# Experts of a decoder block: a float32 second layer from unsplit weights, and 64 rows for the lesser expert of a pair

## The chip, the cores and the metric

One core of a Trainium2 chip runs the whole program; the other cores are idle. The metric is the device time of one execution in microseconds (us), as the median of three runs. Lower is better. The engines are called PE (matrix multiplication), DVE (vector), ACT (scalar), POOL (GpSimd) and SP (which issues most transfers); PEld is PE's loading of stationary operands.

## The reference, cut to what matters

One decoder block on 512 tokens of width 1024: a gated delta-net branch and a dilated attention branch are merged, then comes a mixture of 64 experts, of which each token uses 8, and one shared expert. The change touches the experts alone.

```
scores = sigmoid(h @ w_router); choose 8 experts of each token; wk = their scores, normalised, * 2.5
a = einsum('td,edf->tef', h, w_gate)          # h (512, 1024), w_gate and w_up (64, 1024, 256)
u = einsum('td,edf->tef', h, w_up)
routed = einsum('tef,efd->td', silu(a) * u * combine[..., None], w_down)   # w_down (64, 256, 1024)
out = x + gt2 * (routed + shared)
```

All arrays are float32. An expert's three matrices are 1 MiB each, so that the 64 experts bring 192 MiB (201 MB) from memory in an execution.

## The kernel before, in words

**Precision.** A float32 operand that PE is to multiply is split into a part `hi` of type float32r (a rounded copy, ACT) and a rest `lo` (DVE or POOL, `raw - hi`). A product is then three float32r matmuls: hi·hi, hi·lo and lo·hi. Both layers of an expert work so, lines 1841 to 1843 for the first (gate and up side by side, 512 columns, 8 steps of k, 24 matmuls) and lines 1854 to 1856 for the second (two halves of 512 columns, 2 steps of k, 12 matmuls).

**Jobs.** `make_jobs` (L1657) lays out 36 jobs of up to 128 gathered rows. Experts 0 and 1 have a job each. The other 62 are ranked by their number of tokens, and the most wanted is paired with the least wanted, and so on. The six pairs with the most rows are served by three *triples* of jobs, each with 4 experts and 6 runs of an expert; the other 25 pairs by one job each, with 2 runs. That is 70 runs of an expert (called entries here) with 64 experts' weights. In a pair's job all 128 rows go through both experts, and a row's weight is zero for the expert that it doesn't use.

**The loop.** `run` (L1858) goes through the entries. In entry e PE does, in this order: for the last entry of a job, the eight transposes of the next job's gathered rows (`tile_rows`, L1816); the first five k steps of the first layer; the two transposes of the *previous* entry's result (`mid`, which calls `turned`, L1628); the last three steps; then the second layer of the previous entry (`finish`, `down`, L1846). `turned` writes the transposed result from PSUM twice: ACT copies it to float32r (`hi`) and DVE subtracts to get `lo`, both on line 1638. `gated` (L1620) makes the result from the first layer's PSUM: silu on ACT (L1624), and a product on DVE (L1625).

**Weights.** An expert has six loads of 128x1024 from SP's queue, in order, each into one of ten raw buffers (`raw_tile`). Each part is then cast by ACT and subtracted: first layer L1781 and L1785 (of its four parts one on POOL, three on DVE), second layer L1800 and L1801 (both on DVE). A raw buffer is free for a load when its subtraction is over. The split first-layer weights have two sets of buffers (`wt`, `wy`) for alternate experts, the second layer has two sets as well. The first-layer parts of the second half (j = 1) are split in `mid`, behind `turned`, from the fourth expert on (L1787).

**Rows.** `tile_slot` makes the table of rows of a job: four comparisons with an iota that give one-hots (`slot`, L1649), and four small matmuls (L1653). For the first jobs DVE does the comparisons, from job 6 on POOL does. POOL also issues the gather of rows (L1807) and the scatter that adds a job's result to the output (L1813). `pair_rows` (L1381) gives the rows of a pair their positions, the lesser expert's first.

At the end `overflow` (L2097) runs further jobs, if an expert has more rows than its jobs hold; with these inputs none are needed.

```
au = self.gate_up(x[n], w, mid)
th = self.gated(sw, au, slots[n][1][:, s : s + 1])
if e >= 2 and final[flat[e - 2][2]] == e - 2:
    weights(self.down_weights, flat[e - 2][2] + 2)
if final[w] == e:
    weights(self.gate_up_weights, w + 2)
```

## Time and profile before

| | |
|---|---|
| runs | 1628.46 us median of 3 (1626.53 to 1633.29) |
| the profiled execution | 1629.41 us, its span 1627.6 us |
| PE, PEld busy | 1503.0 us (92%), 1288.1 us (79%) |
| DVE, ACT, POOL busy | 1162.5 us (71%), 847.6 us (52%), 614.2 us (38%) |
| mean granted clock of PE | 0.964 of full speed |
| moved | 344.93 MB, mean 212 GB/s |

A matmul's duration in the profile covers its way through the engine: matmuls overlap, and what one costs in a row of its kind is the distance from its start to the next one's start. A wait is put down to the instruction that ended it. The expert loop begins at 915 us and is the last part of the program.

### The profile page before, as it was taken

What the parts mean: (1) busy time and instruction counts of PE and PEld (TensorE: products, weight loads), DVE (VectorE), ACT (ScalarE), POOL (GpSimd) and SP (SyncE); (2) the same over time, 40 slices, a digit from 0 to 9 for tenths busy, and PEclk for the clock granted to TensorE, in tenths of its full rate; (3) what the DMA queues carried; (4) which work ended last, traced back from release to release, by engine and by line L of the source; (5) the groups of instructions that cost most, each with busy time, mean ns of one, the idle gap of its engine ahead of it and who ended that gap; (6) DMA issues with size and microseconds to landing.
All of it is one profiled execution on the core that took longest, in us unless ns stands there. A gap on an engine that the chain in (4) does not pass through costs nothing.

```text
span 1627.6 us, 25142 instructions
## 1 busy us (share of the span) xinstructions
PE 1503.0 (92%) x8635; PEld 1288.1 (79%) x8635; DVE 1162.5 (71%) x1918; ACT 847.6 (52%) x1697; POOL 614.2 (38%) x422
## 2 busy tenths in 40 slices
PE   4978889899999999999998999899899999998996
PEld 3667778799999999788888777787777877787885
DVE  6678856586655743433477879978998699879885
ACT  5466243544454444323333366657655676656773
POOL 4343121302111111001104397566835594747442
PEclk7999999999999999999997999999999999999998
DMA  8434331323455544233445799999999899989994
GB/s 281 116 99 117 108 87 33 85 91 94 154 146 167 156 135 132 87 101 106 163 142 195 234 291 350 340 326 312 358 317 336 277 351 367 320 293 309 377 375 150
DMA packets 182864, 344.93 MB, mean 212 GB/s; under 512 B 30915, under 2 KB 120206, under 8 KB 182726
## 3 DMA queue, kind: packets, MB, share of 16 engines
q1 hardware_dynamic: 169254, 300.48, 54.0%
q0 software_dynamic: 12672, 40.61, 10.0%
q10 hardware_dynamic: 800, 2.13, 0.3%
q8 instruction: 70, 1.15, 0.3%
q14 instruction: 68, 0.56, 0.1%
HBM read 319.79 MB, written 28.92 MB: 214 GB/s over the span
## 4 chain that ended last, share of the span: by engine, by line
PE 62%; DVE 16%; issue 7%; DMA 6%; ACT 5%; POOL 4%; SPq 0%; POOLq 0%; DVEq 0%; ACTq 0%
PE ps_mm L164 9%; PE ps_mm L165 9%; PE ps_mm L166 9%; PE ps_sm L1841 6%; PE ps_sm L1842 6%; PE ps_sm L1843 6%; DMA gb<-gcd 3%; PE ps_mm L1856 3%; PE ps_mm L1854 3%; PE ps_mm L1855 3%; PE ps_tp L170 2%; DVE lo L1801 2%; PE ps_sm L170 2%; DVE wt L1785 1%; DMA rx<-in_w_exp_up_dram 1%
## 5 line engine op out<-in xcount | busy, mean ns | idle before, releaser
L164 PE MATMUL ps_mm<-hi,hhi 128*128 128x256 f32 x704 | 206.8, 294 | 0.0
L166 PE MATMUL ps_mm<-hi,hlo 128*128 128x256 f32 x704 | 199.8, 284 | 0.0
L165 PE MATMUL ps_mm<-lo,hhi 128*128 128x256 f32 x704 | 199.6, 284 | 0.0
L146 DVE TENSOR_TENSOR lo<-raw,hi 128x1024 fp32r<-128x1024 f32 (+1 forms) x92 | 113.7, 1244 | 109.1 <-ACT hi L144 108.9
L1649 POOL TENSOR_SCALAR oh<-iota,tb 128x128 bf16<-128x128 bf16 x120 | 155.4, 1471 | 0.5
L144 ACT CAST hi<-raw 128x1024 fp32r<-128x1024 f32 (+1 forms) x104 | 103.8, 1014 | 73.7 <-PE ps_mm L165 73.1
L164 PEld LDWEIGHTS ps_mm<-hi,hhi 128*128 128x128 f32 x704 | 135.0, 192 | 3.6 <-PE ps_mm L287 1.3
L1856 PE MATMUL ps_mm<-hi,sw 128*128 128x512 f32 x280 | 114.1, 410 | 24.4 <-DVE sw L1638 24.4
L165 PEld LDWEIGHTS ps_mm<-lo,hhi 128*128 128x128 f32 x704 | 135.1, 192 | 0.1
L164 PE MATMUL ps_mm<-hhi,hi 128*128 128x512 f32 x320 | 132.0, 413 | 3.4 <-DVE cj L563 3.4
L166 PEld LDWEIGHTS ps_mm<-hi,hlo 128*128 128x128 f32 x704 | 134.9, 192 | 0.0
L166 PE MATMUL ps_mm<-hhi,lo 128*128 128x512 f32 x320 | 128.7, 402 | 0.0
L165 PE MATMUL ps_mm<-hlo,hi 128*128 128x512 f32 x320 | 128.3, 401 | 0.0
L1801 DVE TENSOR_TENSOR lo<-rx,hi 128x1024 fp32r<-128x1024 f32 x82 | 114.2, 1427 | 5.0 <-ACT hi L1800 2.7
L1841 PE MATMUL ps_sm<-wt,xh 128*128 128x512 f32 x280 | 117.0, 418 | 0.2 <-ACT xh L1826 0.2
L1842 PE MATMUL ps_sm<-wy,xh 128*128 128x512 f32 x280 | 111.7, 399 | 5.1 <-POOL wy L1785 5.1
L1841 PE MATMUL ps_sm<-wy,xh 128*128 128x512 f32 x280 | 116.2, 415 | 0.0
L1638 ACT CAST sw<-ps_sm 128x256 fp32r<-128x256 f32 x70 | 26.2, 374 | 170.7 <-PE ps_sm L170 168.7
L1842 PE MATMUL ps_sm<-wt,xh 128*128 128x512 f32 x280 | 111.1, 397 | 3.4 <-POOL wt L1785 3.4
L1854 PE MATMUL ps_mm<-hi,sw 128*128 128x512 f32 x280 | 112.3, 401 | 0.5 <-ACT sw L1638 0.5
L1855 PE MATMUL ps_mm<-lo,sw 128*128 128x512 f32 x280 | 112.2, 401 | 0.0
L1843 PE MATMUL ps_sm<-wy,xl 128*128 128x512 f32 x280 | 111.8, 399 | 0.0
(527 smaller groups left out, 4165.1 us busy)
## 6 DMA issues: line engine op xcount, KB each, us to landing
raw<-in_w_in_dram SPq DMA_DIRECT2D x84, 512.0 KB
rx<-in_w_exp_down_dram SPq DMA_DIRECT2D x82, 512.0 KB
rx<-in_w_exp_gate_dram SPq DMA_DIRECT2D x74, 512.0 KB
rx<-in_w_exp_up_dram SPq DMA_DIRECT2D x74, 512.0 KB
raw<-in_w_exp_gate_dram SPq DMA_DIRECT2D x54, 512.0 KB
raw<-in_w_exp_up_dram SPq DMA_DIRECT2D x54, 512.0 KB
raw<-in_w_exp_down_dram SPq DMA_DIRECT2D x46, 512.0 KB
raw<-in_w_ada_dram SPq DMA_DIRECT2D x40, 512.0 KB
```

Source lines behind the costliest of these rows:

```text
L146: eng.tensor_sub(lo[:, s], raw, hi[:, s].bitcast(F32))
L164: nc.tensor.matmul(out, l[0], r[0], start=(k == 0), stop=False)
L165: nc.tensor.matmul(out, l[0], r[1], start=False, stop=False)
L166: return nc.tensor.matmul(out, l[1], r[0], start=False, stop=(k == kd - 1)).ins
L1649: eng.tensor_scalar(oh[:, i, :], iota, col(i)[0], None, op0=ALU.is_equal)
L1801: nc.vector.tensor_sub(dl[:, s], raw, dh[:, s].bitcast(F32))
L1841: nc.tensor.matmul(o, l[0], r[0], start=(k == 0), stop=False)
L1842: nc.tensor.matmul(o, l[0], r[1], start=False, stop=False)
L1843: nc.tensor.matmul(o, l[1], r[0], start=False, stop=(k == KD - 1))
L1854: nc.tensor.matmul(ps[n], hh[0][:, k, :], r[0], start=first and k == 0, stop=False)
L1855: nc.tensor.matmul(ps[n], hh[0][:, k, :], r[1], start=False, stop=False)
L1856: nc.tensor.matmul(ps[n], hh[1][:, k, :], r[0], start=False, stop=last and k == 1)
```

## The change

1. **Second layer.** The weights of the second layer are loaded as they are, in float32, into one of four buffers (`down_tile`; before: two sets of hi and lo). The transposed result is one float32 copy by ACT. The second layer is 4 float32 matmuls in place of 12 float32r ones. ACT's casts and DVE's subtractions of L1800 and L1801 are gone, and so is DVE's `lo` in `turned`.
2. **Lesser expert.** A pair's lesser expert (31 of the 70 entries, `seconds`) has the first 64 rows of its job. `second_rows` (ACT, two copies) puts hi and lo of these 64 rows side by side in one stationary operand of 128 columns. A step of k is then two matmuls: [hi | lo] by the weights' hi, and hi (64 columns) by their lo, 16 in place of 24. The lower 64 PSUM rows are added to the upper ones in `gated_second`: one copy on ACT and two additions on DVE ahead of silu and product. Its `mid` comes after six steps of k.
3. **No tensor work on POOL.** The subtractions and the comparisons that POOL did go to DVE; POOL keeps the gathers and scatters.
4. **Buffers.** Eight raw buffers, for the four loads of the first layer only (before ten, for six). The second layer's loads go straight into `down_tile`.
5. **Rows.** `pair_rows`, `over_rows` and `extra_table` get some small operations on DVE, for pairs whose lesser expert has more than 64 rows.

```diff
     def rest():
-            xl = late.tile([P, 4, 4, P], F32R, name="xl", tag="mT00", bufs=1)
-            self.fx.tiles["xl"] = [xl[:, x] for x in range(4)]
-            rx = late.tile([P, 2, 1024], F32, name="rx", tag="mT01", bufs=1)
-            self.raws[8:10] = [rx[:, x] for x in range(2)]
+            xx = [late.tile([P, 2, 4, 2, P], F32R, name="xx", tag="mT0%d" % x, bufs=1) for x in range(2)]
+            self.fx.tiles["xx"] = [xx[x // 2][:, x % 2] for x in range(4)]
...
+    def gated_second(self, pools, au, comb):
...
+        both = self.fx.tile([P, T], F32, tag="part")[0:M]
+        nc.scalar.copy(both, au[M : 2 * M])
+        for j in range(2):
+            cs = slice(j * 256, j * 256 + 256)
+            nc.vector.tensor_add(both[:, cs], au[0:M, cs], both[:, cs])
+        self.gate_ins = [nc.scalar.activation(th, both[:, 0:256], AF.Silu).ins,
+                         nc.vector.scalar_tensor_tensor(th, th, comb[0:M], both[:, 256:512], op0=ALU.mult,
+                                                        op1=ALU.mult).ins]
...
     def turned(self, pools, th):
...
+        if rows < P:
+            hh = self.fx.tile([P, 2, P], F32, tag="sw_s")
+            pv = ps[:, 0:256].rearrange("p (j t) -> p j t", t=P)[:, :, 0:rows]
+            self.turn_ins = [nc.scalar.copy(hh[:, :, 0:rows], pv).ins]
+            return hh
+        if len(pools) == 2:
+            p, tag, bufs = pools[1]
+            hh = p.tile([P, 2, P], F32, name="sw_f", tag=tag, bufs=bufs)
+            self.turn_ins = [nc.scalar.copy(hh, ps[:, 0:256].rearrange("p (j t) -> p j t", t=P)).ins]
+            return hh
...
+    def down_tile(self, w):
+
+        t = self.wd
+        if t[w % 4] is None:
+            tag = ("hi8", "lo8")[w % 2]
+            t[w % 4] = self.ring.tile([P, 2048], F32, name="wd", tag=tag, bufs=2)
+        return t[w % 4]
 
     def raw_tile(self):
-        n = self.turn
+        x = self.turn % 8
         self.turn += 1
-        x = self.raw_order[n if n < 16 else 16 + (n - 16) % 10]
...
-                    eng = nc.gpsimd if (self.low_pool.pop(0) if self.low_pool else a == 1 and j == 0) else nc.vector
...
-                        eng.tensor_sub(gl, rv, gh.bitcast(F32))
+                        nc.vector.tensor_sub(gl, rv, gh.bitcast(F32))
...
     def down_weights(self, w, load):
-        nc = self.nc
-        dh, dl = self.weight_set(w, 1)
+        d = self.down_tile(w)
         for j in range(2):
-            s = slice(j * 1024, j * 1024 + 1024)
-            raw = self.raw_tile()
-            load(raw, 2, j)
-            with self.tc.issue_after(self.turn_ins[0]) if w >= 2 else ExitStack():
-                nc.scalar.copy(dh[:, s], raw)
-            nc.vector.tensor_sub(dl[:, s], raw, dh[:, s].bitcast(F32))
+            load(d[:, j * 1024 : j * 1024 + 1024], 2, j)
...
+    def second_rows(self, x):
+
+        xs = [self.fx.tile([P, 4, P], F32R, tag="xs") for _ in range(2)]
+        for kk in range(2):
+            self.nc.scalar.copy(xs[kk].rearrange("p k (s r) -> p k s r", s=2), x[kk][:, :, :, 0:M].bitcast(F32))
+        return xs
...
         for k in range(KD):
-            if k == 5:
+            if k == (6 if second else 5):
                 mid()
...
+            if second:
+                xk = x[k // 4][:, k % 4]
+                parts = [(o, xk, r[0]), (o[0:M], xk[:, 0:M], r[1])]
+                for m, (oo, l, rr) in enumerate(parts if k < KD - 1 else parts[::-1]):
+                    nc.tensor.matmul(oo, l, rr, start=(k + m == 0), stop=(k + m == KD))
+                continue
...
     def down(self, ps, hh, w, first, last):
...
-        for n in range(2):
-            for k in range(2):
+        for k in range(2):
+            for n in range(2):
                 c = k * D + n * 512
-                r = [d[s][:, c : c + 512] for s in range(2)]
-                nc.tensor.matmul(ps[n], hh[0][:, k, :], r[0], start=first and k == 0, stop=False)
-                nc.tensor.matmul(ps[n], hh[0][:, k, :], r[1], start=False, stop=False)
-                nc.tensor.matmul(ps[n], hh[1][:, k, :], r[0], start=False, stop=last and k == 1)
+                nc.tensor.matmul(ps[n], hh[:, k, :], d[:, c : c + 512], start=first and k == 0, stop=last and k == 1)
...
+            if e + 1 < len(flat) and flat[e + 1][2] in seconds and not w in seconds:
+                xs = self.second_rows(x[flat[e + 1][0]])
...
-            au = self.gate_up(x[n], w, mid)
-            th = self.gated(sw, au, slots[n][1][:, s : s + 1])
+            second = w in seconds
+            au = self.gate_up(xs if second else x[n], w, mid, second)
+            th = (self.gated_second if second else self.gated)(sw, au, slots[n][1][:, s : s + 1])
+            if second and e + 1 < len(flat) and flat[e + 1][2] in seconds:
+                xs = self.second_rows(x[flat[e + 1][0]])
...
-                    later.append(self.tile_slot(n + 4, nc.gpsimd))
+                    later.append(self.tile_slot(n + 4, nc.vector))
...
+        seconds = [NS + x for x, u in enumerate(self.pairs) if u >= NQ]
+        self.run([ws for _, ws in self.jobs], prepare, load, ahead, between, seconds)
```

## Rows read from the trace of the kernel before

**Rows 1.** The busy time of each engine in eight stretches (the windows view; the columns stand in its first line). The first seven lie end to end and are the expert loop from the first matmul of job 2 to that of job 35: five pairs, the first triple of jobs, six pairs, the second triple, six pairs, the third triple, seven pairs. The eighth is a part of the seventh.

```profile
944.40:1047.30 102.90, 94.65 (x448) 76.83 (x448) 94.68 (x94) 67.17 (x93) 77.64 (x45) 0.95 0.97 335
1047.30:1101.40 54.10, 54.10 (x267) 44.51 (x267) 41.74 (x53) 32.42 (x47) 33.99 (x24) 1.00 0.94 317
1101.40:1224.40 123.00, 114.72 (x548) 92.32 (x548) 114.07 (x146) 80.36 (x111) 77.49 (x45) 0.97 0.96 334
1224.40:1284.00 59.60, 55.97 (x270) 45.58 (x268) 43.42 (x55) 33.38 (x48) 36.30 (x27) 0.97 0.90 301
1284.00:1400.00 116.00, 110.86 (x531) 89.70 (x529) 107.51 (x117) 79.96 (x111) 80.54 (x49) 0.99 0.99 354
1400.00:1459.80 59.80, 56.39 (x270) 45.63 (x269) 43.67 (x48) 33.64 (x48) 30.87 (x20) 0.97 0.90 289
1459.80:1590.40 130.60, 126.33 (x593) 104.17 (x591) 117.23 (x132) 91.45 (x124) 69.33 (x35) 0.97 0.99 350
1520.00:1580.00 60.00, 60.00 (x283) 49.96 (x282) 52.34 (x60) 44.83 (x59) 25.00 (x12) 1.00 1.03 375
```

**Rows 2.** The timeline of PE: the first first-layer matmul of job 7 (where the first triple begins) and of job 10 (after it), of job 20 and of job 21 (two pairs in a row). Columns: start in us, duration in us, engine, line, operation, operands.

```profile
1047.35 0.48 PE L1841 MATMUL ps_sm<-wt,xh 128*128 128x512 f32 x1
...
1101.46 0.48 PE L1841 MATMUL ps_sm<-wt,xh 128*128 128x512 f32 x1
...
1302.03 0.48 PE L1841 MATMUL ps_sm<-wt,xh 128*128 128x512 f32 x1
...
1320.07 0.47 PE L1841 MATMUL ps_sm<-wt,xh 128*128 128x512 f32 x1
```

**Rows 3.** Who waited for whom from 944.4 to 1590.4 us (the waits view): PE's two largest, and two of SP's, the queue that issues the weight loads.

```profile
PE ps_mm L1856 <- DVE sw L1638: 24.4, 10, 4.6
PE ps_sm L1842 <- POOL wy L1785: 4.5, 2, 3.6
...
SPq L1989 <- DVE lo L1801: 119.5, 104, 7.0
...
SPq L1989 <- POOL wy L1785: 73.0, 22, 7.1
```

**Rows 4.** One of the stalls in the timeline (DVE, POOL and PE, 973 to 984 us); in square brackets the idle time before the instruction and what ended it.

```profile
973.01 2.99 POOL L1785 TENSOR_TENSOR wt<-rx,wt 128x1024 fp32r<-128x1024 f32 x1 [1.49 <-ACT wt L1781]
974.07 4.15 DVE L1801 TENSOR_TENSOR lo<-raw,hi 128x1024 fp32r<-128x1024 f32 x2
...
981.67 0.41 DVE L1638 TENSOR_TENSOR sw<-ps_sm,sw 128x256 fp32r<-128x256 f32 x1
...
982.13 0.80 PE L1856 MATMUL ps_mm<-hi,sw 128*128 128x512 f32 x1 [3.69 <-DVE sw L1638]
...
983.15 0.63 PE L1855 MATMUL ps_mm<-lo,sw 128*128 128x512 f32 x1
983.58 0.63 PE L1856 MATMUL ps_mm<-hi,sw 128*128 128x512 f32 x1
```

**Rows 5.** One line's instructions over the whole run (the source view): shortest, median and longest duration in ns. First DVE's subtraction of a 128x1024 first-layer weight part, then the comparison that makes a one-hot, on POOL and on DVE.

```profile
L1785 DVE TENSOR_TENSOR wt<-rx,wt x55: 1206/1224/4007, 922.2 to 1588.7; 128x1024 fp32r<-128x1024 f32 x55
...
L1649 POOL TENSOR_SCALAR oh<-iota,tb x120: 590/1321/5112, 933.6 to 1480.6; 128x128 bf16<-128x128 bf16 x120
L1649 DVE TENSOR_SCALAR oh<-iota,tb x24: 239/246/255, 895.0 to 930.0; 128x128 bf16<-128x128 bf16 x24
```

**Rows 6.** Groups of instructions from 944.4 to 1590.4 us, shapes kept apart (the lines view): busy time in us, mean ns of one, and idle time before them with what ended it.

```profile
L1801 DVE TENSOR_TENSOR lo<-rx,hi 128x1024 fp32r<-128x1024 f32 x74 | 104.8, 1449 | 2.3 <-ACT hi L1800 2.3
...
L1785 DVE TENSOR_TENSOR wt<-rx,wt 128x1024 fp32r<-128x1024 f32 x54 | 87.5, 1644 | 4.5 <-ACT wt L1781 4.5
...
L1781 ACT CAST wy<-rx 128x1024 fp32r<-128x1024 f32 x68 | 68.6, 1053 | 1.6 <-DMA rx<-in_w_exp_up_dram 0.9 <-DMA rx<-in_w_exp_gate_dram 0.7
...
L1826 ACT CAST xh<-ps_tp 128x512 fp32r<-128x512 f32 x66 | 35.8, 589 | 13.7 <-PE ps_tp L170 13.7
...
L1625 DVE SCALAR_TENSOR_TENSOR sw_t<-sw_t,cmb,ps_sm 128x256 f32<-128x256 f32 x66 | 31.1, 471 | 5.0 <-ACT sw_t L1624 5.0
...
L1638 DVE TENSOR_TENSOR sw<-ps_sm,sw 128x256 fp32r<-128x256 f32 x66 | 27.5, 417 | 55.6 <-ACT sw L1638 51.9 <-issue 3.7
...
L1624 ACT ACTIVATE sw_t<-ps_sm 128x256 f32<-128x256 f32 x66 | 25.2, 382 | 7.9 <-PE ps_sm L1843 7.9
```

**Rows 7.** The timeline of PE, for the spacing of matmuls that follow each other: the first and the last of the 12 float32r matmuls of an entry's second layer, 512 columns each, and three records of float32 matmuls with 256 columns in the attention (line 967; each program matmul of that line leaves two such records).

```profile
1062.55 0.39 PE L1854 MATMUL ps_mm<-hi,sw 128*128 128x512 f32 x1
...
1065.04 0.39 PE L1856 MATMUL ps_mm<-hi,sw 128*128 128x512 f32 x1
...
426.90 0.38 PE L967 MATMUL ps_sm<-dk,dq 128*128 128x256 f32 x1
...
427.12 0.38 PE L967 MATMUL ps_sm<-dk,dq 128*128 128x256 f32 x1
...
427.33 0.38 PE L967 MATMUL ps_sm<-dk,dq 128*128 128x256 f32 x1
```

**Rows 8.** What the DMA engines moved (the DMA view), from 944.4 to 1590.4 us and from 1520 to 1580 us.

```profile
DMA packets 60145, 214.72 MB, mean 332 GB/s; under 512 B 7833, under 2 KB 7833, under 8 KB 60090
...
DMA packets 6348, 22.52 MB, mean 375 GB/s; under 512 B 861, under 2 KB 861, under 8 KB 6341
```

**Rows 9.** PE's largest wait from 915 to 944.4 us, in the first two jobs (the waits view).

```profile
PE ps_tp L1653 <- POOL oh L1649: 2.5, 2, 2.2
```

More of the change, by code (lines that the diff above doesn't have):

```diff
@@ L22 @@
 KD = D // P
+M = 64
 NT = T // P
@@ L1630, in turned @@
         ps = self.ps_sm()
+        rows = th.shape[0]
         for j in range(2):
-            self.transpose(ps[:, j * P : (j + 1) * P], th[:, j:256:2])
+            self.transpose(ps[:, j * P : j * P + rows], th[:, j:256:2])
+        if rows < P:
[8 more added lines that the diff above has]
+            return hh
         p, tag, bufs = pools[1]
@@ L1729, in expert_tiles @@
         rx = [late.tile([P, 2, 1024], F32, name="rx", tag="mT1%d" % x, bufs=1) for x in range(2)]
-        self.raws = [rx[x // 2][:, x % 2] for x in range(4)] + [None] * 6
-        self.raw_order = (0, 1, 2, 3, 4, 5, 6, 7, 0, 1, 2, 3, 4, 5, 8, 9, 0, 1, 6, 7, 2, 3, 4, 5, 8, 9)
+        self.raws = [rx[x // 2][:, x % 2] for x in range(4)] + [None] * 4
         self.turn = 0
-        self.low_pool = [1, 1, 1, 1, 0, 1, 0, 1]
-        sw = late.tile([P, 2, 2, 2, P], F32R, name="sw", tag="wr", bufs=1)
-        self.fx = Fixed({"xh": [late.tile([P, 4, P], F32R, name="xh", tag="gt%d" % (x // 2), bufs=2) for x in range(4)],
-                         "xl": [], "sw_h": [sw[:, 0, x] for x in range(2)], "sw_l": [sw[:, 1, x] for x in range(2)]})
-        self.fx.turn["xl"] = 0
+        sw = late.tile([P, 4, 2, P], F32, name="sw", tag="wr", bufs=1)
+        nc.gpsimd.memset(sw[:, 2:4], 0.0)
+        self.fx = Fixed({"part": [late.tile([P, T], F32, name="part", tag="gt0", bufs=2) for _ in range(2)],
+                         "xs": [late.tile([P, 4, P], F32R, name="xs", tag="gt1", bufs=2) for _ in range(2)],
+                         "sw_f": [sw[:, x] for x in range(2)], "sw_s": [sw[:, 2 + x] for x in range(2)]})
+        self.fx.turn["xx"] = 0
         self.xg = []
@@ L1767, in gate_up_weights @@
         nc = self.nc
-        g = self.weight_set(w, 0)
+        g = self.weight_set(w)
         for j in range(2):
@@ L1818, in tile_rows @@
         nc = self.nc
-        xh, xl = [[self.fx.tile([P, 4, P], F32R, tag=tag) for _ in range(2)] for tag in ("xh", "xl")]
+        xx = [self.fx.tile([P, 4, 2, P], F32R, tag="xx") for _ in range(2)]
         for kk in range(2):
@@ L1825, in tile_rows, with gate_up @@
             p3 = pt.rearrange("p (k t) -> p k t", t=P)
-            nc.scalar.copy(xh[kk], p3)
-            nc.vector.tensor_sub(xl[kk], p3, xh[kk].bitcast(F32))
-        return xh, xl
-    def gate_up(self, x, w, mid):
+            nc.scalar.copy(xx[kk][:, :, 0], p3)
+            nc.vector.tensor_sub(xx[kk][:, :, 1], p3, xx[kk][:, :, 0].bitcast(F32))
+        return xx
+    def second_rows(self, x):
[3 more added lines that the diff above has]
+        return xs
+    def gate_up(self, x, w, mid, second=False):
         nc = self.nc
-        g = self.weight_set(w, 0)
+        g = self.weight_set(w)
         au = self.ps_sm()
@@ L1848, in down, with run @@
         nc = self.nc
-        d = self.weight_set(w, 1)
-        for n in range(2):
-            for k in range(2):
+        d = self.down_tile(w)
+        for k in range(2):
+            for n in range(2):
                 c = k * D + n * 512
-                r = [d[s][:, c : c + 512] for s in range(2)]
-                nc.tensor.matmul(ps[n], hh[0][:, k, :], r[0], start=first and k == 0, stop=False)
-                nc.tensor.matmul(ps[n], hh[0][:, k, :], r[1], start=False, stop=False)
-                nc.tensor.matmul(ps[n], hh[1][:, k, :], r[0], start=False, stop=last and k == 1)
-    def run(self, tiles, prepare, load, ahead=lambda n: None, between=(None,) * 4):
+                nc.tensor.matmul(ps[n], hh[:, k, :], d[:, c : c + 512], start=first and k == 0, stop=last and k == 1)
+    def run(self, tiles, prepare, load, ahead=lambda n: None, between=(None,) * 4, seconds=()):
         nc = self.nc
@@ L1869, in run @@
         slots, rows, x, out = {}, {}, {}, {}
-        sw = ((self.ring, "acc", 2), (self.fx, "sw_h", 2), (self.fx, "sw_l", 2))
+        sw = ((self.ring, "acc", 2), (self.fx, "sw_f", 2))
         def begin(n):
@@ L1973, in ahead @@
                 with self.tc.issue_after(self.gather_ins):
-                    later.append(self.tile_slot(n + 4, nc.gpsimd))
+                    later.append(self.tile_slot(n + 4, nc.vector))
             if n == 16:
                 self.extra_table()
-        self.run([ws for _, ws in self.jobs], prepare, load, ahead, between)
+        seconds = [NS + x for x, u in enumerate(self.pairs) if u >= NQ]
+        self.run([ws for _, ws in self.jobs], prepare, load, ahead, between, seconds)
         self.overflow()
@@ L2008, in extra_table @@
         ps = self.ps_tp()
-        nc.tensor.matmul(ps[0:NQ, 0:1], cu, self.onesb[:, 0:1], start=True, stop=True)
+        for s in range(2):
+            nc.tensor.matmul(ps[0:NQ, 3 * s : 3 * s + 1], cu[:, s], self.onesb[:, 0:1], start=True, stop=True)
         for s in range(2):
```

64 lines of the change are left out of this document (41 added, 23 removed).

## The prediction, made before the changed kernel was run

> **What bounds the kernel now.** I read the expert loop alone, since the edits lie there. The windows view first [rows 1]: over the seven stretches from 944.4 to 1590.4 us (24 pairs and three triples, 646.0 us) PE is busy for 613.0 us, DVE for 562.3 (90 to 93% in the runs of pairs), and the DMA share is 0.90 to 0.99. Three resources look nearly full, so the shares don't say which one sets the pace. The timeline does. Two jobs in which PE never waits start at 1302.03 and 1320.07 us, so that a pair costs PE 18.04 us; the first triple goes from 1047.35 to 1101.46 us, 54.11 us [rows 2]. At that pace the loop takes 24 x 18.04 + 3 x 54.11 = 595.3 us. The 50.7 us above it are what PE loses.
>
> To whom, the waits view says [rows 3]: 24.4 us to DVE's `lo` of a transposed result (10 times, up to 4.6 us), and smaller sums to POOL's subtractions. No transfer stands there. SP, in its turn, waits for DVE's and POOL's subtractions (119.5 and 73.0 us in two of its rows), so the loads wait for raw buffers, not the splits for loads. One stall shows the mechanism [rows 4]: POOL subtracts from 973.01 to 976.00 us, and DVE's two subtractions beside it take 4.15 us together; the `lo` that PE needs is reached at 981.67, and PE, idle for 3.69 us, goes on at 982.13. Its next matmuls stand 0.43 us apart (983.15, 983.58), against 0.226 us in [rows 7]: they run at 1.2 GHz, the lower of the two levels. So a stall costs more than its wait, and 50.7 is more than the waits' sum.
>
> Why DVE is late: its subtraction takes 1224 ns at the median but up to 4007 [rows 5], and in the loop two of the six groups have means of 1449 and 1644 ns over 74 and 54 instructions [rows 6]; against 1220 that is 17 + 23 = 40 us of blocking in these two. DVE is full in the pairs because of second-layer subtractions and because POOL's tensor work holds it up.
>
> **The change, part by part.**
>
> *Second layer in float32.* The 12 matmuls of an entry start from 1062.55 to 1065.04 us, 0.226 us apart, and take 2.72 us [rows 7]. A float32 matmul of 256 columns leaves two records, each 0.215 us from the next (426.90, 427.12, 427.33): two cycles per column and record. With 512 columns that is 2 x 0.43 = 0.86 us, and four make 3.44 us. So PE pays 0.72 us more per entry.
> The Trainium skill ("FP8 and Floating Point Precision", "TensorE Precision Notes") counts four passes for true float32; with four passes at 0.226 us the matmul would be 0.90 us, which would add 0.04 x 4 x 66 = 11 us to the sum as an estimate. The row is the float32 matmul itself, and I take the row.
>
> *Lesser expert.* 8 of 24 matmuls fall away in each of these entries: 8 x 0.226 = 1.81 us less. A stationary operand of 64 columns I price like one of 128; nothing in these rows makes it dearer.
>
> *PE's sum.* A pair: 18.04 + 2 x 0.72 - 1.81 = 17.67 us. A triple has six entries, two of them lesser: 54.11 + 4.32 - 3.62 = 54.81 us. The loop's floor becomes 24 x 17.67 + 3 x 54.81 = 588.5 us, 6.8 less than before. The two halves nearly cancel on PE; what matters is the rest.
>
> *DVE and POOL.* In the eighth stretch, where POOL makes no more one-hots, DVE is busy for 52.34 of 60 us [rows 1], 15.5 us per 17.8 us of a pair. Per pair the change takes away four second-layer subtractions (4.9 us at 1.22) and two `lo` of a result (0.8 us at 417 ns), and adds two first-layer subtractions that were POOL's (2.4 us), four one-hots at 246 ns (1.0 us) [rows 5, 6] and two additions over 64 rows (at most 0.8 us). That is 14.0 us of 17.67, and the blocking by POOL's subtractions is over, as nothing is left there but descriptors. So the stalls of [rows 4] should go. ACT loses four casts of 1.05 us per pair and gets two row copies and one PSUM copy of at most 0.59 us: not a bound.
>
> *The lesser expert's result* has a longer way: PSUM copy 0.59, two additions 0.83, silu 0.38, product 0.47 [rows 6], 2.3 us, before its transposes. They are due after the previous entry's second layer and five k steps, 3.44 + 15 x 0.226 = 6.8 us. Queued ahead may be the two casts (2.1 us) and two subtractions (2.4 us) of the pending split: also 6.8 us in all. I take 0, and keep the case below.
>
> *Transfers* are now the next in line. The loop moved 214.72 MB; the best long stretch ran at 375 GB/s [rows 8]. At that rate the loop's bytes take 572.6 us, under PE's 588.5, but the two don't meet at every moment. An expert is 3 MiB; the loop's 60 experts are 188.7 MB, and the other 26 MB are 0.79 per job. So a pair (7.08 MB) takes 18.9 us against 17.67 and falls 1.2 us behind, while a triple (14.95 MB, 39.9 us) wins 15 us. In front of this stands the lead of the buffers: with eight for four loads an expert, a raw buffer is free two entries before its data is due (with ten for six loads, some one and a half). That is 17.7 us, of which an expert's transfer (8.4) and its splits (3) leave about 6. A run of five to seven pairs falls behind by 6 to 8.5 us, so 0 to 3 us are lost in each of the four. I take 13 us in all, as the 375 GB/s were reached with many loads queued. The ends are 0, and no lead at all: at 375 GB/s 24 x 18.9 + 3 x 54.81 = 618 us, 30 lost, and at the 354 GB/s of the fastest run of pairs now [rows 1] 24 x 20.0 + 164.4 = 644, 56 lost.
> By the Trainium skill ("SBUF — State Buffer", "SBUF: two separate sides") a core gets about 358 GB/s from HBM; the loop's bytes would then need 600 us as an estimate, 11 over the floor. The 375 GB/s of 60 us exceed that figure, so the row decides; the rule's direction is that of the first rival.
>
> *Before and after the loop.* In the first two jobs POOL's one-hots cost PE 2.5 us [rows 9], which go; six subtractions of the first experts move from POOL to DVE (7 us) while four of the second layer go (5 us); `pair_rows` and `over_rows` get eight small operations. Between -5 and +7 us, mostly beside the routing; I take 0. The last two entries lie outside the loop: -0.4 us, and up to 3 for a stall.
>
> **The sum.** 646.0 becomes 588.5 + 13 = 601.5: 44.5 us less, and 0.4 at the end. The profiled execution took 1629.41 us, 0.95 over the median of the runs; 1628.5 - 44.9 = 1583.6 us.
>
> **The rivals.**
>
> *Transfers take over.* The share of 0.97 to 0.99 at 334 to 354 GB/s in the pairs [rows 1] speaks for it; that hardly an engine waits for data now, the ACT cast of one group for 1.6 us in all [rows 6], speaks against. With no lead, and a rate midway between 354 and 375 GB/s, a pair takes 19.4 us and the loop 24 x 19.4 + 164.4 = 630 us: 1612 us, still faster.
>
> *DVE stays late.* The work is in order, and 14.0 us of 17.67 can still put a `lo`-like product behind a subtraction. If all 50.7 us stayed, only PE's 6.8 would be won: 1622 us. Against it: PE's transposed result no longer needs DVE at all. DVE's remaining link is the product, due later.
>
> *The lesser expert's result comes late* (slower). Place: PE at `mid` after each of the 31 lesser entries. If one more cast and subtraction (1.05 + 1.22) stand ahead, the 6.8 us become 9.1, 2.3 over the cover of 6.8, and a stall at half clock is longer than its wait. 31 x 2.3 = 71 us: 1655 us. It decides the sign from 45 / 31 = 1.5 us per entry. For it: both queues are in order, and the pending split is issued just before. Against: DVE and ACT have more idle time than before.
>
> *The change doesn't do what it says*, if the lesser expert had more than 64 rows in a pair, and further jobs had to run. Before, no job ran in the overflow, so pairs hold 128 rows at most and the lesser half is 64 at most: I give it nothing.
>
> **How the numbers follow.** Forecast 0.65 (1563 to 1600), transfers 0.17 (1600 to 1625), DVE 0.10 (1605 to 1628), the late result 0.08. The low end is the floor without loss, with 5 less at the start and 3 at the end: 1628.5 - 57.5 - 8 = 1563. The high end takes in the transfers' own time of 1612 and stops at 1614, as beyond it lie the late result and the worse halves of the two other cases, 0.2 in all. About 0.5% (8 us) is what a measurement of this kernel can tell from no change. Faster: 0.65, 0.15 of the transfers and 0.04 of DVE, 0.84. Within it: 0.02 and 0.06, 0.08. Slower: 0.08.
>
> **What would show it.** Second-layer records: 8 per entry, 0.43 us apart, an entry's second layer 3.4 us. Lesser entries: 16 first-layer matmuls at 0.23. Hardly a DVE subtraction over 1.3 us. POOL with descriptors alone. A pair at 17.7 us where PE doesn't wait, the loop near 600 us; the 24.4 us of waiting for `lo` gone, and waits for weights in its place, late in the runs of pairs. Wrong would be: float32 records more than 0.45 us apart, PE waiting at the transposes of lesser entries, or pairs that stay over 19 us.

## The result and the profile after

| | before | after | forecast for after |
|---|---|---|---|
| median of the runs, us | 1628.16 (1626.53 to 1633.29, 4 runs) | 1588.09 (1586.63 to 1590.54, 4 runs) | 1583.6 (1563 to 1614) |
| ratio to before, 95% interval | | 0.9748 [0.9730, 0.9766] | |
| profiled execution / its span, us | 1629.41 / 1627.6 | 1590.54 / 1588.8 | |
| expert loop, job 2 to job 35, us | 646.0 | 601.3 | 601.5 |
| start of job 2 in the span, us | 944.45 | 950.12 | as before |
| from job 35 to the end, us | 37.1 | 37.4 | 0.4 less |

The change is 2.5% faster. The loop came out within 0.2 us of its forecast, but not by the forecast's terms: the floor was 9.5 us higher and the loss 9.7 us lower, and the experiments show that one of the three parts, POOL's work, brings 35 of the 40 us when it alone is taken out of the kernel before. The stretches and starts of a kernel are those of its one profiled execution, which is the slowest of the four runs in after, the fastest of ten in e1 and of five in e5.

The windows view of after, with the stretches of [rows 1]: five pairs, a triple, six pairs, a triple, six pairs, a triple, seven pairs, and in the eighth line 60 us of the seventh. The columns are stretch, length, busy time of PE, PEld, DVE, ACT and POOL with instruction counts, PE's granted clock, DMA share, GB/s.

```profile
950.10:1039.70 89.60, 89.60 (x367) 57.53 (x364) 68.65 (x111) 57.54 (x88) 16.20 (x11) 1.00 1.03 378
1039.70:1095.30 55.60, 55.60 (x227) 36.38 (x226) 33.54 (x55) 26.98 (x43) 9.07 (x6) 1.00 0.94 333
1095.30:1205.10 109.80, 109.80 (x452) 70.16 (x451) 86.38 (x165) 70.70 (x109) 15.22 (x11) 1.00 1.02 372
1205.10:1260.70 55.60, 55.52 (x230) 36.58 (x228) 34.45 (x57) 27.10 (x44) 10.98 (x7) 1.00 0.93 326
1260.70:1368.60 107.90, 107.90 (x438) 69.08 (x435) 83.12 (x131) 69.84 (x109) 17.04 (x12) 1.00 1.02 376
1368.60:1424.30 55.70, 55.55 (x228) 36.46 (x225) 34.22 (x51) 27.48 (x44) 8.72 (x5) 1.00 0.89 312
1424.30:1551.40 127.10, 126.36 (x489) 79.83 (x487) 92.00 (x124) 80.27 (x121) 19.47 (x13) 1.00 1.01 369
1480.00:1540.00 60.00, 59.86 (x227) 37.96 (x226) 39.90 (x48) 35.15 (x53) 8.06 (x5) 1.00 1.02 375
```

PE is now busy for 600.3 of the 601.3 us and at the full clock. DVE, over 90% busy in the pairs before, is at 72 to 79%. The DMA share is 1.01 to 1.03 in the pairs, at 369 to 378 GB/s: the transfers look like a second resource without room, though e5 below shows that some is left.

The chain at one pair, in after's timeline of PE (start, duration, engine, line, operation, operands; x8 counts records that stand close together): the pair's first matmul, the greater entry's second layer, the first 12 first-layer matmuls of the lesser entry, and the next pair's first matmul.

```profile
1260.70 0.48 PE L1895 MATMUL ps_sm<-wt,xx 128*128 128x512 f32 x1
...
1266.87 3.59 PE L1907 MATMUL ps_mm<-wd,sw 128*128 128x512 f32 x8
...
1271.09 3.03 PE L1892 MATMUL ps_sm<-wy,xs 128*128 128x512 f32 x12
...
1278.66 0.47 PE L1895 MATMUL ps_sm<-wt,xx 128*128 128x512 f32 x1
```

The pair takes 17.96 us. The eight float32 records span 3.59 us, the last of them 0.59: seven spacings of 0.43 us. The three triples take 55.6 to 55.8 us, so that the floor is 24 x 17.96 + 3 x 55.7 = 598 us, and 3 us of the loop are lost: some 2 us in the two pairs from 1149.20 to 1187.15 us, where PE also does the matmuls of the table for further jobs, and some 2 us in the last pair, which is 20.16 us long (1531.29 to 1551.45). Other pairs near the end are a little shorter than 17.96 us.

DVE's first-layer subtractions in after's source view (shortest, median, longest in ns), and the groups of POOL in the loop (lines view: busy us, mean ns, idle before), where [rows 5, 6] had up to 4007 ns and POOL's tensor work:

```profile
L1828 DVE TENSOR_TENSOR wt<-rx,wt x128: 1203/1219/1227, 866.7 to 1554.1; 128x1024 fp32r<-128x1024 f32 x128
L1828 DVE TENSOR_TENSOR wy<-raw,wy x128: 1204/1218/1228, 888.1 to 1564.9; 128x1024 fp32r<-128x1024 f32 x128
```

```profile
L1850 POOL DMA_INDIRECT out_dram<-y,idx x34 | 57.4, 1689 | 260.0 <-DVE y L1943 249.8 <-DVE xx L1864 4.9 <-DVE o_cu L2066 4.4
L1844 POOL DMA_INDIRECT xg<-h2d,idx x31 | 39.3, 1266 | 240.9 <-PE ps_tp L171 175.7 <-PE ps_sm L171 54.7 <-issue 9.3
```

All 256 subtractions now take 1.20 to 1.23 us: the blocking is gone. PE's 24.4 us of [rows 3] have no successor; the waits view of the loop holds one wait of PE:

```profile
PE ps_mm L1907 <- ACT sw L1671: 0.2, 1, 0.2
```

Before the loop there is a new one (waits view, 944.4 to 950.2 us), in the place of [rows 9]: the transposes of job 2's rows wait for their gather, which POOL issued at 935.59 us.

```profile
PE ps_tp L171 <- DMA xg<-h2d,idx: 6.2, 1, 6.2
```

### The profile page after: what moved, and what is told of

The parts are those of the page before. It is cut to its first block, busy times and chain, and to the rows that moved or that the text cites. A ratio compares the mean times of both kernels' runs of the same rounds, so it can differ in the third digit from the quotient of the medians.

```text
span 1588.8 us, 23505 instructions
## 1 busy us (share of the span) xinstructions
PE 1493.4 (94%) x8108; PEld 1173.6 (74%) x8108; DVE 1023.4 (64%) x1983; ACT 780.4 (49%) x1662; POOL 282.2 (18%) x235
## 4 chain that ended last, share of the span: by engine, by line
PE 75%; DVE 10%; DMA 6%; ACT 4%; issue 2%; POOL 2%; SPq 0%; POOLq 0%; DVEq 0%; ACTq 0%
PE ps_mm L1907 14%; PE ps_mm L165 9%; PE ps_mm L166 9%; PE ps_mm L167 9%; PE ps_sm L1892 7%; PE ps_sm L1895 5%; PE ps_sm L1896 4%; PE ps_sm L1897 4%; DMA gb<-gcd 4%; PE ps_tp L171 3%; PE ps_sm L171 2%; DVE cy L495 1%; DVE bp L657 1%; DVE lo L147 1%; PE ps_sm L1002 1%
## 5 line engine op out<-in xcount | busy, mean ns | idle before, releaser
L1907 PE MATMUL ps_mm<-wd,sw 128*128 128x512 f32 x560 | 254.0, 595 | 0.6 <-ACT sw L1666 0.4
L1828 DVE TENSOR_TENSOR wt<-rx,wt 128x1024 fp32r<-128x1024 f32 x128 | 152.7, 1220 | 67.6 <-ACT wt L1825 67.0
L1828 DVE TENSOR_TENSOR wy<-raw,wy 128x1024 fp32r<-128x1024 f32 x128 | 153.6, 1218 | 55.5 <-ACT wy L1825 54.9
L1907 PEld LDWEIGHTS ps_mm<-wd,sw 128*128 128x128 f32 x560 | 105.9, 190 | 106.4 <-issue 92.5
L1825 ACT CAST wt<-rx 128x1024 fp32r<-128x1024 f32 x128 | 129.8, 1047 | 8.7 <-DMA rx<-in_w_exp_gate_dram 5.8
L1825 ACT CAST wy<-raw 128x1024 fp32r<-128x1024 f32 x128 | 129.6, 1048 | 4.6 <-DMA raw<-in_w_exp_gate_dram 2.9
L1892 PE MATMUL ps_sm<-wy,xs 128*128 128x512 f32 x448 | 119.7, 408 | 0.6 <-DVE wy L1828 0.6
L1850 POOL DMA_INDIRECT out_dram<-y,idx x36 | 61.3, 1703 | 287.4 <-DVE y L1943 277.2
L1895 PE MATMUL ps_sm<-wt,xx 128*128 128x512 f32 x256 | 107.5, 420 | 0.4 <-ACT wt L1825 0.4
L1896 PE MATMUL ps_sm<-wt,xx 128*128 128x512 f32 x256 | 100.5, 393 | 0.9 <-DVE wt L1828 0.8
L1897 PE MATMUL ps_sm<-wt,xx 128*128 128x512 f32 x256 | 100.6, 393 | 0.0
```

The costliest lines, as they stand in the source:

```text
L1825: nc.scalar.copy(gh, rv)
L1828: nc.vector.tensor_sub(gl, rv, gh.bitcast(F32))
L1892: nc.tensor.matmul(oo, l, rr, start=(k + m == 0), stop=(k + m == KD))
L1895: nc.tensor.matmul(o, l[0], r[0], start=(k == 0), stop=False)
L1896: nc.tensor.matmul(o, l[0], r[1], start=False, stop=False)
L1897: nc.tensor.matmul(o, l[1], r[0], start=False, stop=(k == KD - 1))
```

## The experiments

Ratios are to the kernel before, run on the same chip.

| label | kernel | us | ratio [95%] |
|---|---|---|---|
| | after | 1588.1 | 0.9748 [0.9730, 0.9766] |
| e1 | after, lesser expert with 128 rows | 1629.1 | 1.0001 [0.9992, 1.0011] |
| e2 | after, POOL's tensor work put back | 1605.7 | 0.9845 [0.9822, 0.9868] |
| e3 | e1 and e2 together: only float32 is left | 1630.5 | 1.0014 [1.0004, 1.0025] |
| e4 | after, second layer split again | 1604.8 | 0.9847 [0.9830, 0.9863] |
| e12 | e2 and e4 together: only the 64 rows are left | 1709.4 | 1.0478 [1.0445, 1.0512] |
| e9 | before, POOL's tensor work given to DVE | 1593.3 | 0.9782 [0.9755, 0.9808] |
| e10 | after, POOL's subtractions put back | 1603.1 | 0.9838 [0.9812, 0.9863] |
| e11 | after, POOL's one-hots put back | 1588.7 | 0.9748 [0.9721, 0.9774] |
| e5 | after, lesser expert's transposes from 128 rows | 1576.9 | 0.9680 [0.9666, 0.9693] |
| e6 | after, load order at the start | 1593.2 | 0.9766 [0.9739, 0.9793] |
| e7 | e5 and e6 together | 1581.6 | 0.9704 [0.9682, 0.9726] |
| e8 | after, a sixth of the weight bytes left out | 1583.0 | 0.9719 [0.9705, 0.9733] |

### e1: the lesser expert with 128 rows

```
-        seconds = [NS + x for x, u in enumerate(self.pairs) if u >= NQ]
+        seconds = []
```

> The changed kernel with the lesser expert's 64 rows undone: it runs 128 rows and 24 first-layer matmuls like the other, float32 second layer and the idle POOL stay. Theory (PE sets the pace now): each of the 31 lesser entries gets 8 x 0.226 = 1.81 us longer and loses the 0.31 us at its transposes, so a pair goes from 17.96 to 19.46 us, and 31 x 1.50 = 46.5 us come on top of 1588.1: 1635 us (1628 to 1642), with gaps shorter than now, as the transfers (18.9 us a pair) get time. Rival (the gain came from DVE and POOL being relieved, PE has room): below 1605 us.

Measured: 1629.1 us, the time before. In the timeline of PE the starts of two neighbouring pairs stand 19.45 us apart:

```profile
1276.60 0.48 PE L1895 MATMUL ps_sm<-wt,xx 128*128 128x512 f32 x1
...
1296.05 0.47 PE L1895 MATMUL ps_sm<-wt,xx 128*128 128x512 f32 x1
```

Its loop takes 642.8 us, all of it PE's (busy for 642.76), 41.5 us more than after's 601.3. So PE sets the pace of the changed kernel, and the 64-row edit is worth 1.49 us per pair. The total is 6 us below the middle of what was expected. In the loop, which holds 30 of the 31 lesser entries, 45.0 us were expected and 41.5 came: the 3 us that after's loop loses are not lost here. The rest stays open: the profiled loop starts at 943.75 us, 6 us before after's, but the two profiled executions lie 3.4 us under and 2.5 us over the medians of their kernels.

### e2, e10, e11: POOL's tensor work put back

```
-                        nc.vector.tensor_sub(gl, rv, gh.bitcast(F32))
+                        eng = nc.gpsimd if (self.low_pool.pop(0) if self.low_pool else a == 1 and j == 0) else nc.vector
+                        eng.tensor_sub(gl, rv, gh.bitcast(F32))
...
-                    later.append(self.tile_slot(n + 4, nc.vector))
+                    later.append(self.tile_slot(n + 4, nc.gpsimd))
```

e2 has both hunks, e10 the first alone, e11 the second.

> The changed kernel with tensor work put back on POOL: one of four first-layer subtractions of each expert and the four one-hots of a job, as before the change; float32 second layer and 64-row lesser expert stay. Theory (POOL's blocking cost time only because DVE was full): DVE has 13 of 18 us of work per pair, loses some 3.4 us of it and gets about 1.7 us of blocking, so PE goes on at 17.96 us per pair: 1585 to 1598 us, longer DVE subtractions (up to 4 us) again, but hardly a wait of PE. Rival (the blocking by POOL was itself the loss of about 40 us): over 1615 us, PE waiting for DVE's and POOL's subtractions.

> The changed kernel with only the first-layer subtractions put back on POOL (one of four of each expert); the one-hots stay on DVE. Both parts together cost 17.6 us. If it is the long subtraction, which blocks DVE's beside it and comes late itself, this run carries most of it: 1597 to 1606 us, with DVE subtractions of up to 4 us. If it is the one-hots, which come late for the gathers: 1588 to 1593 us.

> The changed kernel with only the one-hots put back on POOL; the subtractions stay on DVE. By the theory that the long subtraction is what costs, 1587 to 1594 us; by the rival that the one-hots do, 1597 us or more, with PE or POOL waiting for slots and gathers.

Measured: 1605.7 us for both, between theory and rival, which both failed: the room on DVE doesn't make the blocking free. The subtractions alone bring 15.0 of the 17.6 us, the one-hots 0.6, inside the measurement. How a subtraction still reaches PE stands in e10's timeline, at a greater entry (DVE, then POOL, then PE):

```profile
1266.79 2.65 DVE L1645 SCALAR_TENSOR_TENSOR sw_t<-sw_t,cmb,part 64x256 f32<-64x256 f32 x1
```

```profile
1266.21 2.94 POOL L1830 TENSOR_TENSOR wy<-raw,wy 128x1024 fp32r<-128x1024 f32 x1 [4.84 <-ACT wy L1826]
```

```profile
1269.59 0.42 PE L171 MATMUL ps_sm<-ident,sw_t 64*128 64x64 f32 x2 [0.28 <-DVE sw_t L1645]
```

The product of the lesser expert's result, which takes 0.47 us in after, lasts 2.65 us: it ends at 1269.44, 0.29 after POOL's subtraction ends at 1269.15. PE's transposes wait for it. This is the blocking itself, on a small instruction on the path. The Trainium skill ("SBUF — State Buffer", "SBUF: two separate sides") says that a GpSimd instruction and a DVE instruction with two inputs in SBUF, the on-chip memory, don't share their common port: the one that starts first holds it for its whole length; the 2.65 us agree.

The greater expert's product is spared. One of its operands comes straight from PSUM, where matmuls write, while the lesser's both lie in SBUF since `gated_second` adds up there (e10, source views of both lines, ns):

```profile
L1645 DVE SCALAR_TENSOR_TENSOR sw_t<-sw_t,cmb,part x31: 467/2370/2653, 967.9 to 1582.8; 64x256 f32<-64x256 f32 x31
L1654 DVE SCALAR_TENSOR_TENSOR sw_t<-sw_t,cmb,ps_sm x39: 467/475/483, 926.4 to 1573.3; 128x256 f32<-128x256 f32 x39
```

So the 64-row edit itself put an instruction on PE's path that POOL can hold up. It explains a part: of the 9.9 us that PE waits in e10's loop (612.6 us, 11.3 more than after's), 3.3 are waits for this product, ten times; the others are smaller waits, for POOL's own subtractions among them.

### e3: only the float32 second layer

Both edits (e1's and e2's) together.

> Both of these at once: the lesser expert with 128 rows and POOL's tensor work as before the change, so that of the three parts only the float32 second layer is left. Theory: PE's pair is 19.46 us and DVE has about 11 us of work in it, so POOL's work hides as well: 1632 to 1645 us, that is no gain over before, since float32 costs PE 0.72 us an entry and buys DVE room that PE then doesn't use. Rival (the parts add up, each with its own gain): the float32 layer alone is worth a gain of 10 us or more over the 1628 us of before.

Measured: 1630.5 us, as the theory has it. PE is busy for 642.76 of the loop's 644.2 us, DVE for 347.5. Float32 alone leaves DVE busy for 54% of the loop, and makes PE so long that nothing is won.

### e4, e12: the second layer split again

```
-            load(d[:, j * 1024 : j * 1024 + 1024], 2, j)
+            raw = self.raw_tile()
+            load(raw, 2, j)
+            nc.scalar.copy(dh[:, s], raw)
+            nc.vector.tensor_sub(dl[:, s], raw, dh[:, s].bitcast(F32))
...
-                nc.tensor.matmul(ps[n], hh[:, k, :], d[:, c : c + 512], start=first and k == 0, stop=last and k == 1)
+                nc.tensor.matmul(ps[n], hh[0][:, k, :], r[0], start=first and k == 0, stop=False)
+                nc.tensor.matmul(ps[n], hh[0][:, k, :], r[1], start=False, stop=False)
+                nc.tensor.matmul(ps[n], hh[1][:, k, :], r[0], start=False, stop=last and k == 1)
```

e12 has e2's two hunks as well.

> The changed kernel with the second layer back in 12 float32r matmuls from weights that ACT and DVE split (six loads an expert through eight raw buffers, where before had ten); 64-row lesser expert and idle POOL stay. Theory (float32 is paid on PE and repaid on DVE): PE's pair falls to 18.0 - 1.44 = 16.5 us, but DVE gets four subtractions of 1.22 us and two of 0.42 us per pair more, some 19.5 us, and sets the pace: 24 x 19.5 us and triples of 55 us make a loop of 635 to 660 us, 1622 to 1650 us in all, PE waiting for DVE in every pair. Rival (PE alone counts, float32 is a loss): 70 x 0.72 = 50 us less than the changed kernel, about 1540 us.

> The changed kernel with both the split float32r second layer and POOL's tensor work as before, so that of the three parts only the 64-row lesser expert is left (with eight raw buffers for ten). Theory (DVE full and blocked): PE's sum is 16.5 us per pair, DVE's 16.1 us plus some 1.7 us of blocking, so DVE sets the pace and the stalls stay: 1600 to 1625 us. Rival (the lesser expert's 1.5 us per entry are won whatever DVE does): 1628 - 46 = 1582 us.

Measured: e4 1604.8 us. Neither range holds it, but the theory has the direction: its loop takes 628.5 us although PE has less to do, DVE is busy for 581.2 of them, and PE waits for DVE and ACT (waits view, 942 to 1571 us):

```profile
PE ps_mm L1909 <- DVE y L1947: 9.9, 6, 4.2
PE ps_mm L1909 <- ACT sw L1674: 9.4, 7, 2.7
PE ps_sm L1897 <- DVE wt L1823: 8.1, 9, 1.9
```

So beside a short lesser expert float32 wins 16.7 us. Some of them may be buffers: e4 has two raw buffers less than before, and for hi and lo of the transposed result one buffer each for greater and for lesser entries, where before had two for all. The 19.5 us per pair that were expected of DVE were a sum of durations; its busy time is 103.9 us over six late pairs, 17.3 each: the records of neighbouring DVE instructions overlap (two subtractions in a row take 2.36 us, not 2.44), and only one job's one-hots are left in this stretch.

e12: 1709.4 us, 81 more than before and 105 more than e4, far outside both ranges. PE waits for POOL's subtractions themselves (waits view, 946 to 1668 us), and its mean granted clock falls to 0.92 in the loop:

```profile
PE ps_sm L1899 <- POOL wt L1825: 39.7, 10, 10.0
PE ps_sm L1895 <- POOL wy L1825: 24.7, 16, 6.6
PE ps_sm L171 <- DVE sw_t L1645: 15.1, 5, 4.6
PE ps_sm L1895 <- POOL wt L1825: 7.1, 3, 2.5
```

How much of the 105 us belongs to the buffers (eight raw ones for six loads, where before had ten, and the single ones of the transposed result) stays open; e4 lives with the same.

### e9: the kernel before without POOL's tensor work

```
-                    eng = nc.gpsimd if (self.low_pool.pop(0) if self.low_pool else a == 1 and j == 0) else nc.vector
+                    eng = nc.vector
...
-                    later.append(self.tile_slot(n + 4, nc.gpsimd))
+                    later.append(self.tile_slot(n + 4, nc.vector))
```

> The kernel before with only POOL's tensor work (first-layer subtractions and one-hots) given to DVE; split second layer and 128-row lesser expert stay. Theory (a pair costs the larger of PE's and DVE's sums): DVE's sum goes from 15.5 to 18.9 us per pair and is freed of the blocking, PE's is 18.04; 24 x 18.9 and three triples of 54 us, with about 8 us of stalls, make a loop of 624 us: 1600 to 1615 us. Rival (POOL's share was needed, since DVE is the fullest engine): 1628 us or more.

Measured: 1593.3 us, below the expected range: two small edits to the kernel before bring 35 us. Its loop takes 605.1 us (947.8 to 1552.9) against 646.0, on the old floor of 595.3: 9.8 us lost instead of 50.7. The subtractions of one tile in the source view (900 to 1600 us), and in the windows view two pairs of 18.04 us and six pairs:

```profile
L1785 DVE TENSOR_TENSOR wt<-rx,wt x72: 1201/1222/1247, 917.5 to 1553.1; 128x1024 fp32r<-128x1024 f32 x72
```

```profile
1427.82:1463.89 36.07, 36.07 (x181) 29.67 (x179) 33.50 (x48) 25.89 (x37) 7.00 (x5) 1.00 0.98 335
1261.67:1369.90 108.23, 108.23 (x533) 88.90 (x531) 104.69 (x146) 81.13 (x112) 25.48 (x12) 1.00 1.00 364
```

PE waits for nothing there although DVE is busy for 33.50 of 36.07 us (93%) and for 104.69 of 108.23 (97%). DVE has up to 17.4 us of work per pair, not the 18.9 expected. Over the whole loop it does POOL's subtractions and one-hots as well, 808 instructions instead of 638 (windows views of the two loops), and is yet busy for 559.5 us instead of 562.3: its busy time before held the time in which it was blocked, and the move takes this away.

### e5: the lesser expert's transposes from 128 rows

```
-        th = p.tile([P, 256], F32, name="sw_t", tag=tag, bufs=bufs)[0:M]
-        both = self.fx.tile([P, T], F32, tag="part")[0:M]
+        part = self.fx.tile([P, T], F32, tag="part")
+        both = part[0:M]
+        th = both[:, 0:256]
...
-        return th
+        return part[:, 0:256]
...
-            self.transpose(ps[:, j * P : j * P + rows], th[:, j:256:2])
+            self.transpose(ps[:, j * P : (j + 1) * P], th[:, j:256:2])
...
+        for x in self.fx.tiles["part"]:
+            nc.gpsimd.memset(x[M:P, 0:256], 0.0)
```

`turned` gets the number of rows as an argument.

> The changed kernel with one edit: the lesser expert's result is formed inside the 128-row tile of its partial sums, whose lower half is zeroed once, and its two transposes read 128 rows instead of 64; all else stays. Theory (the 64-row transposes themselves cost the time, by a break in PE's pipeline where their form differs from the matmuls around them): the step at which they stand in greater entries falls from 0.70 to 0.39 us, a pair from 17.96 to 17.65 us, 31 x 0.31 = 9.6 us; as a pair's loads need more time than that, up to half may come back as waits for weights: 1577 to 1584 us. Rival (PE waits there for the lesser expert's late product, which the trace doesn't record as a wait): the step stays at 0.70 us, 1587 to 1589 us.

Measured: 1576.9 us, 11 less than after, the fastest kernel of the study. The place in after (PE, then its weight loads), and the same place in e5:

```profile
1263.98 0.39 PE L1897 MATMUL ps_sm<-wt,xx 128*128 128x512 f32 x1
1264.30 0.45 PE L171 MATMUL ps_sm<-ident,sw_t 64*128 64x64 f32 x2
1264.68 0.50 PE L1895 MATMUL ps_sm<-wt,xx 128*128 128x512 f32 x1
```

```profile
1264.30 0.31 PEld L171 LDWEIGHTS ps_sm<-ident,sw_t 64*128 64x128 f32 x2 [0.35 <-issue]
```

```profile
1253.18 0.40 PE L1899 MATMUL ps_sm<-wt,xx 128*128 128x512 f32 x1
1253.42 0.39 PE L171 MATMUL ps_sm<-ident,part 128*128 128x128 f32 x2
1253.57 0.48 PE L1897 MATMUL ps_sm<-wt,xx 128*128 128x512 f32 x1
```

From the matmul before to the matmul behind it takes 0.70 us in after and 0.39 in e5. The product was not late: it ended at 1262.3 us, two us ahead. What held PE is the form of the two transposes, 64 rows by 64 columns; which of the two it is, e5 doesn't separate, as it changes both. Its loop takes 589.3 us, 12 less than after's, in an execution 4.4 us under e5's median.

### e6, e7: the load order at the start

```
-            if e >= 2 and final[flat[e - 2][2]] == e - 2:
-                weights(self.down_weights, flat[e - 2][2] + 2)
+            kinds = [(self.down_weights, flat[e - 2][2] + 2)] if e >= 2 and final[flat[e - 2][2]] == e - 2 else []
             if final[w] == e:
-                weights(self.gate_up_weights, w + 2)
+                kinds.insert(0 if e == 2 else 1, (self.gate_up_weights, w + 2))
+            for kind in kinds:
+                weights(*kind)
```

The expert numbers of four experts in place of two are kept for it. e7 adds e5's edit.

> The changed kernel with one edit: at the third entry the loads of expert 4's first layer are issued before those of expert 2's second layer (whose buffer comes free only with the last shared expert's matmuls), so that SP doesn't stand 21 us before them. Theory (the weight loads that pile up behind that wait, from 935.8 us, slow the gather that job 2's transposes wait for): the 6.2 us wait for the gather falls to 0 to 2 us and the loop starts 4 to 6 us sooner: 1582 to 1585 us. Rival (the start is late by DVE's longer queue, the gather is only the last to be seen): the gather's wait turns into one for DVE or ACT, 1587 to 1589 us.

> Both edits together, the 128-row transposes and the load order. If they are independent the gains add: 1588 - 9.6 - 5 = 1573 to 1579 us. If the transfers have become the bound, the sum of the two is short by what the loop waits for weights, and it stays at 1580 to 1584 us.

Measured: 1593.2 and 1581.6 us; no gain (e6's runs spread from 1579.9 to 1594.6). The four loads do go out earlier, from 924.64 us, but the gather still comes late (waits view, 925 to 950 us):

```profile
PE ps_tp L171 <- DMA xg<-h2d,idx: 4.7, 1, 4.7
```

Both expectations fail. From the gather's issue to the transposes it took 8.1 us in before, 9.9 in after, 7.5 in e5, 8.3 in e6, 5.4 in e4; the weight loads of this order aren't what decides it. The cause stays open.

### e8: a sixth of the weight bytes left out

```
-        for j in range(2):
+        for j in range(2 if w < 4 else 1):
             load(d[:, j * 1024 : j * 1024 + 1024], 2, j)
```

> The changed kernel with a sixth of the weight bytes left out: from expert 4 on only half of the second layer's weights is loaded, the other half of the matmuls uses what an earlier expert left in the buffer (so the result isn't the reference's). A pair's bytes fall from 7.08 to 6.03 MB, 16.1 us at 375 GB/s, below PE's 17.96. Theory (the transfers cost little now, at the ends of the runs of pairs, in the last two jobs and in the gather before job 2): 8 to 16 us less, 1572 to 1580 us, and no waits for weights at the end. Rival (the transfers set the pace of the pairs): a pair falls below 17.96 us and the total by more than 25 us. A second rival (transfers are hidden throughout): 1586 to 1589 us.

Measured: 1583.0 us, 5 less than after and between the two theories that count small; the loop takes 597.6 us instead of 601.3, that is the floor, and from job 35 to the end 35.8 instead of 37.4. At 314 GB/s over the loop the waits view has no wait of PE for weights. Of the 3.7 us in the loop, 2.4 are the last pair's: 20.16 us in after, 17.76 in e8. So in after the transfers cost some 5 us by the medians; the intervals of the two ratios just touch.

## Why the prediction came out, and by which of its steps

The three parts as a cube, in us; the last column is DVE's busy time as a share of the loop in the kernel without POOL's work:

| second layer, lesser expert | POOL works | POOL idle | POOL's work costs | DVE busy |
|---|---|---|---|---|
| split, 128 rows | 1628.2 (before) | 1593.3 (e9) | 35 | 559.5 / 605.1 = 0.92 |
| split, 64 rows, eight raw buffers | 1709.4 (e12) | 1604.8 (e4) | 105 | 581.2 / 628.5 = 0.92 |
| float32, 128 rows | 1630.5 (e3) | 1629.1 (e1) | 1 | 411.0 / 642.8 = 0.64 |
| float32, 64 rows | 1605.7 (e2) | 1588.1 (after) | 18 | 432.4 / 601.3 = 0.72 |

- **What bounded the kernel**: right. PE's pace was 595.3 us, and 50.7 us were lost to DVE's lateness behind POOL's subtractions; e9 takes away 41 of them with nothing but POOL's work.
- **Which part cures it**: the prediction named two reasons for DVE's lateness, the second layer's subtractions and POOL's blocking, and didn't weigh them. They are two cures for one loss. In before POOL's is enough: e9 has 35 of the 40 us, and float32 with 64 rows adds some 5 (ratios 0.9782 and 0.9748, whose intervals overlap). With POOL at work, float32 and 64 rows bring 23 us (e2). Neither of these two is seen to be a gain alone: float32 +2 us (e3), 64 rows +81 (e12, which also has fewer buffers than before; 64 rows with before's buffers were not run).
- **Float32**: 3.44 us per entry, as priced. The Trainium skill's four passes ("FP8 and Floating Point Precision", "TensorE Precision Notes") at 0.226 us gave 0.90 us per matmul; the records give 2 x 0.43 = 0.86, so the row was the better price.
- **Lesser expert**: its entry takes 7.57 us against 9.39 with 128 rows in e1, the 1.81 that was priced. The step that failed is what the prediction didn't cost at all: the 64-row transposes, 0.31 us for each of the 31 lesser results, 9.6 us. "Nothing in these rows makes it dearer" held for the matmuls with 64 columns and wasn't asked of the transposes with 64 rows. With that mended, e5's loop of 589.3 us, in that one execution, stands on the predicted floor of 588.5.
- **DVE's 14.0 us per pair**: 83.12 / 6 = 13.9 in the fifth stretch.
- **The lesser expert's late result**, the slower rival: it doesn't happen. The product is two us early at the place shown above, and PE never waits for it in after's loop; it takes POOL's subtraction beside it (e10) to make it late.
- **Transfers**: mis-sized. 13 us were taken, although the prediction's own working, 0 to 3 us in each of four runs of pairs, gave 12 at most; some 4 are lost in the loop, most of them in its last pair, and 1.5 behind it (e8). The pairs run at 369 to 378 GB/s, as the best 60 us of [rows 8] did, and the lead of the buffers holds until the last pair. The figure of about 358 GB/s in the Trainium skill ("SBUF — State Buffer", "SBUF: two separate sides"), which it works out as half of 716 GB/s for two cores, would have given 600 us for the loop's bytes. The 601.3 us look like it, by chance: e5 moves the same bytes in 589.3 us, at 366 GB/s, with no other core at work.
- **The start**: 0 was taken, the profiled execution shows 5.7 us. This execution lies 2.5 us over after's median, and job 2 starts between 942.2 and 950.1 us in the kernels here; job 0, ahead of nearly all that was changed, alone varies by 5 us. What belongs to the change isn't settled.

So the sum came out because the 9.6 us of the transposes and the 9 us too many for the transfers cancel. That the loop came out to 0.2 us is luck. The direction and the mechanism were right, two terms were not.

## What to carry to other kernels

Where one engine blocks another, the victim's busy time holds the blocking: moving the blocker's work to the victim can relieve it, and here POOL's subtractions and one-hots, given to a DVE at over 90%, won 35 us. Price such a move by the undisturbed durations (1.22 us here), not by the busy share. When two edits cure the same stall, their gains don't add and one of them may be a loss alone; run the cheap one by itself first. And when a tile gets fewer rows, price every instruction that reads it, the transposes too.

## What the runs showed of the hardware

- **The transposes of 64 rows cost PE extra, the stationary operands of 64 columns do not.** Two transposes of 64 rows (and 64 moving columns) between matmuls of 128 rows hold PE for 0.70 us, of 128 rows (and 128 columns) for 0.39; the weight load stands idle for 0.35 us ahead of them, with no wait recorded. In the lesser entries stationary operands of 128 and of 64 columns take turns, eight times each, at 0.23 us a matmul as elsewhere. The Trainium skill ("TensorEngine Tiling (Array Packing)", "Key Properties") says that a change of the tiling mode drains TensorE. If both forms count as such modes here, which no run settles, the rows form agrees at some 0.3 us and the columns form shows nothing of it.
- **A POOL subtraction can lengthen DVE instructions whose operands all lie in SBUF; none with an operand in PSUM was lengthened here.** In before, DVE's `lo` of the second-layer weights (both operands in SBUF) takes up to 4.3 us, its `lo` of the transposed result (one operand in PSUM) never over 0.43 (source views of before):

```profile
L1801 DVE TENSOR_TENSOR lo<-rx,hi x82: 1205/1216/4324, 902.4 to 1605.6; 128x1024 fp32r<-128x1024 f32 x82
L1638 DVE TENSOR_TENSOR sw<-ps_sm,sw x70: 405/417/426, 938.5 to 1611.0; 128x256 fp32r<-128x256 f32 x70
```

  The same holds in e2, e10 and e12. So before's `lo` of the result was late by the queue ahead of it, not by itself.
- **What POOL's work costs is not read off DVE's share.** It is 1 us in all with DVE at 0.64 of the loop, 18 at 0.72, but 35 and 105 in two kernels at 0.92, for some 60 subtractions with means of 2.6 to 3.1 us (and the one-hots, which e11 finds free). These kernels also differ in what stands on PE's path: the lesser expert's product is there in e2 and e12, and not in e3. In e3 no DVE subtraction takes over 1.38 us, so little collided at all; why isn't shown.
